# Starting the head mixing of an mLSTM layer at the first half of value chunk 0 instead of its second half

## The chip, the cores and the metric

The kernel runs on one core of one Trainium2 chip. The metric is the device time of one execution in microseconds. Engines are named as in the profile: PE (matrix products), PEld (its weight loads), DVE (elementwise work), ACT (activations and copies), POOL, and SP (which issues most transfers). Each engine works through its own instructions in the order in which the program lists them; semaphores hold an instruction back until what it needs is done.

## The reference

A trunk of two layers on 256 tokens of width 2048. The change lies in the second layer, an mLSTM with 8 heads (key width 128, value width 256):

```python
u = hn @ o_w_in[j]                      # q and k (2048), v (2048), og (2048), z (2048), gates (16)
qk = jax.nn.silu(causal_conv(qk, c_conv_w[j], c_conv_b[j]))
li = ig + c_b_i[j]
lf = jax.nn.log_sigmoid(fg + c_b_f[j])
yc = mlstm(q, k, v, li, lf)             # per head: exp-weighted causal q k^T, times v, with a normaliser
yc = head_rmsnorm(yc, c_norm[j]) * jax.nn.sigmoid(og) * jax.nn.silu(z)
h = h + yc @ o_w_out[j]
```

The kernel does the recurrence as one full causal product per head: scores q k^T, weighted by exponentials of gate sums, then times v. Products in 32-bit precision are made of three reduced-precision products of a high part ("hi") and a rest ("lo") of each operand.

## The kernel before

**Weight products.** Each projection is cut into chunks of 512 columns. `seven` (L288) makes two chunks at a time, with a Strassen-like scheme of seven products on the first quarter of the rows and plain products on the other three. It is a generator; it holds four PSUM banks A, F, B (pool `pm`, tile name `mm`, three banks) and E (pool `px`, name `mx`, three banks) and works through a string of operations, `a5a6.2aA7b.4F.bb`. `a` and `b` are plain products of 24 matmuls (`plain`), a digit is one Strassen product of 6, a dot is a call of `pump`, and `A` and `F` hand the first and the second half (128 tokens each) of the first chunk to the caller; E and B follow at the end as the halves of the second chunk. Ahead of the string stand two products of 6, into A and then into E. Three passes matter here: pass 1 is `seven(a["ov"], 0, ...)` for value chunks 0 and 1, pass 2 `seven(a["ov"], 2, ...)` for value chunks 2 and 3, pass 3 the first of the output gate, on `in_oog_dram`. All these matmuls are recorded at L235 (`product`). The first matmul of every product is tied by `tc.issue_after(last["pe"])` to stand behind the last matmul of the product before it, so the products never change places among themselves. Weights come through raw buffers; ACT makes the hi part (`whi`, L137 or L221), DVE the lo part (`wlo`, L138 or L222), in four buffers each.

**Lanes.** Other work hangs in named lanes, each a queue of generators. `pump` (L77) takes one step of each lane; it is called in the middle of each `plain` and at each dot. `drain` runs a lane to its end at once. The framework's scheduler then settles, when the program is built, in which order each engine's instructions stand: in general as they were written, earlier ones or those under `high_priority` first, and an instruction that needs a buffer stands behind those whose buffer it takes over.

**The lanes here.** `qk0` to `qk3` hold `features(t, j)` (L1196): convolution and SiLU of the q and k chunks, on DVE at L1218 (taps) and L1222, and on ACT at L1221 (`th`, the tanh). Lane `mix` holds `gate_stats` (L1256; it ends in eight small transposes `aT<-ae` at L1285), then `mix(0)` to `mix(3)` (two heads each) and `mix_norm`. One `mix(j)` consists of these steps, a step for each `pump`:

1. "spread": two PE matmuls (L431) broadcast a row of gate maxima over a bank `mx`; DVE subtracts it (`wt`, L1305 and L1306), ACT takes exponentials (L1310, L1311).
2. hi and lo parts of q and k (`qhl`, `khl`; ACT L1322, DVE L1323). `khl` lies in tag `th` of pool `tp`, two buffers that it shares with the `th` of `features`. For j = 0 there is one idle step ahead of this.
3. "scores": six matmuls L1329 and two L1330 into two banks `mx`; DVE multiplies them into `wt` (L1331); ACT makes `sh` (L1334), DVE `sl` (L1335).
4. "nu": 18 matmuls L1349 of `sh`/`sl` with the value tiles `vt`/`vl` of chunk j, into two banks `mx` and two `st`; then copies, row sums and squares (L1352, L1353, L1355). The next `mix` begins in the same step with its spread.

`px` has three banks. They go round in the order of the code: E of a pass, spreads, scores and two of the four nu banks all take their turn.

**Where the change acts.** `values` (L1386) takes the halves that passes 1 and 2 hand out, scales them into `vt` and `vl` (ACT L1394, DVE L1395), and at one of them puts `mix(0)` to `mix(3)` and `mix_norm` into their lane.

Of the kernel before, what the change touches and what calls it, by code (L numbers as in the profile page):

```python
# [45 lines left out]
def trunk(ctx: ExitStack, tc: tile.TileContext, a, out):  # L46
# [19 lines left out]
    def start(lane, gen):  # L66
        lanes.setdefault(lane, []).append(gen)
# [16 lines left out]
    def drain(*which):  # L84
        for lane in which:
            while step(lane):
                pass
# [687 lines left out]
    if True:  # L775
# [283 lines left out]
        vts = []  # L1059
# [133 lines left out]
    with tc.tile_pool(name="m1", bufs=2) as m1:  # L1193
# [50 lines left out]
        vts = []  # L1244
# [113 lines left out]
        def mix_norm():  # L1358


            t, r, yh = (m1.tile([P, 16], F32, name=n, bufs=1) for n in ("nwt", "nwr", "nwy"))
            s.activation(den, den, AF.Abs)
            v.tensor_tensor(out=den.rearrange("p (h n) -> p h n", h=2), in0=den.rearrange("p (h n) -> p h n", h=2),
                            in1=aT[:, 1, :, 0:8], op=ALU.max)
            v.tensor_scalar(den, den, 1e21, EPS ** 0.5, op0=ALU.min, op1=ALU.mult)
            v.tensor_tensor(out=den, in0=den, in1=den, op=ALU.mult)
            v.scalar_tensor_tensor(den, ss, 1.0 / 256, den, op0=ALU.mult, op1=ALU.add)
            newton(den, t, r, yh)
            for hf in range(2):
                c = slice(hf * 8, hf * 8 + 8)  # L1370
                v.tensor_scalar(fac[:, c], r[:, c], 0.5, None, op0=ALU.mult)
            yield
# [4 lines left out]
        def value_halves():  # L1377
            drain("combos")
            pr = pieces(m1.tile([P, 1024], F32, name="pr", tag="vt", bufs=6))
            yield from seven(a["ov"], 0, acth, qs, (0,), chain, pr, acc=True)  # L1380
            drain("spill")
            store_of.extend(hp.tile([P, 1024], F32, name="pr", tag="h") for _ in range(2))
            for b, hf, src in seven(a["ov"], 2, acth, qs, (0,), chain, part, acc=True):
                yield 2 + b, hf, src

        def values():  # L1386
            for j, hf, src in value_halves():
                if hf == 0:
                    vt = m1.tile([P, 2, 2, VW], F32R, name="vt", tag="vt", bufs=6)
                    gp.memset(vt.bitcast(F32)[:, :, :, 256:VW], 1.0)  # L1390
                    vl = ap.tile([P, 1024], F32R, name="vl", tag="ahl").rearrange("p (h i e) -> p h i e", h=2, i=2)
                with tc.high_priority(offset=450):
                    src = src.rearrange("p (i e) -> p i e", i=2)
                    s.activation(vt[:, hf, :, 0:256], src, AF.Copy, scale=norm["rt"][:, hf:hf + 1])  # L1394
                    v.scalar_tensor_tensor(vl[:, hf], src, norm["rt"][:, hf:hf + 1], vt[:, hf, :, 0:256].bitcast(F32),  # L1395
                                           op0=ALU.mult, op1=ALU.subtract)
                if hf == 0:
                    continue
                vts.append((vt, vl))
                if j == 0:  # L1400
                    drain("qk0", "qk2")
                    for c in range(4):
                        start("mix", mix(c))
                    start("mix", mix_norm())
# [18 lines left out]
        def mixed_gates():  # L1423
            for j, th in [x for x in held if x[0] in nums]:
                v.scalar_tensor_tensor(nums[j], th, 1.0, nums[j], op0=ALU.add, op1=ALU.mult)
            held[:] = [x for x in held if x[0] not in nums]

        values()
        for jj in (0, 2):
            ths = [m1.tile([P, 2, 512], F32, name="tho", tag="vt", bufs=6) for _ in range(2)]  # L1430
# [10 lines left out]
        for jj in (0, 2):  # L1441
            us = [m1.tile([P, 2, 512], F32, name="u", tag="vt", bufs=6) for _ in range(2)]
            for b, hf, src in pair(a["oz"], jj, True):
                j, u = jj + b, us[b]
# [292 lines left out]
```

## Time and profile before

| what | value |
|---|---|
| median of 3 runs | 1028.01 us (1027.76 to 1029.28) |
| the profiled execution | 1028.51 us |
| its span, first to last instruction | 1026.7 us |
| PE busy | 1011.9 us of the span |
| DVE, ACT, POOL busy | 850.5, 665.8, 103.5 us |
| HBM traffic | 236 GB/s over the span |

Start and launch around the span make up the 1.8 us between the first two profiled figures. The median of the runs lies 0.5 us under the profiled execution. In the timeline a row gives the start, the length, the engine, the line, the operation, and in brackets how long the engine had been idle and who released it. Instructions of one engine overlap by a little, so the distance between two starts is what one costs in a sequence.

### The profile page before, as it was taken

What the parts mean: (1) busy time and instruction counts of PE and PEld (TensorE: products, weight loads), DVE (VectorE), ACT (ScalarE), POOL (GpSimd) and SP (SyncE); (2) the same over time, 40 slices, a digit from 0 to 9 for tenths busy, and PEclk for the clock granted to TensorE, in tenths of its full rate; (3) what the DMA queues carried; (4) which work ended last, traced back from release to release, by engine and by line L of the source; (5) the groups of instructions that cost most, each with busy time, mean ns of one, the idle gap of its engine ahead of it and who ended that gap; (6) DMA issues with size and microseconds to landing.
All of it is one profiled execution on the core that took longest, in us unless ns stands there. A gap on an engine that the chain in (4) does not pass through costs nothing.

```text
span 1026.7 us, 14530 instructions
## 1 busy us (share of the span) xinstructions
PE 1011.9 (99%) x5152; PEld 838.6 (82%) x5152; DVE 850.5 (83%) x1242; ACT 665.8 (65%) x956; POOL 103.5 (10%) x184
## 2 busy tenths in 40 slices
PE   9999999999999999999999999899999999999996
PEld 8888888888888888878888877688888888888886
DVE  7858968969686888879579998778989997899794
ACT  7775554686974555567557877676666867465562
POOL 0111101011111111022021100000011110111000
PEclk9999999999999999999999999899999999999998
DMA  9987756567688799588897856447879889686852
GB/s 360 335 223 250 222 175 203 167 200 238 221 263 303 246 298 286 165 263 254 290 314 217 263 166 219 163 155 204 251 194 296 237 236 354 198 284 210 283 184 83
DMA packets 69960, 243.18 MB, mean 237 GB/s; under 512 B 9056, under 2 KB 10464, under 8 KB 69888
## 3 DMA queue, kind: packets, MB, share of 16 engines
q1 hardware_dynamic: 55872, 197.56, 57.5%
q0 software_dynamic: 13584, 44.18, 16.4%
q8 instruction: 40, 0.66, 0.3%
q10 hardware_dynamic: 432, 0.52, 0.1%
q14 instruction: 32, 0.26, 0.1%
HBM read 222.31 MB, written 19.92 MB: 236 GB/s over the span
## 4 chain that ended last, share of the span: by engine, by line
PE 89%; DVE 7%; issue 1%; ACT 1%; DMA 1%; ACTq 0%; DVEq 0%; POOLq 0%
PE mm L235 27%; PE mm L211 12%; PE mm L213 12%; PE mm L212 12%; PE mx L235 8%; PE mx L213 3%; PE mx L212 3%; PE mx L211 3%; DVE wlo L138 2%; DVE qk L1218 2%; DVE wlo L222 1%; PE mm L517 1%; PE nu L1349 1%; PE mx L517 1%; PE mm L1562 1%
## 5 line engine op out<-in xcount | busy, mean ns | idle before, releaser
L138 DVE TENSOR_TENSOR wlo<-raw,whi 128x1024 fp32r<-128x1024 f32 (+1 forms) x305 | 366.1, 1211 | 101.8 <-ACT whi L137 96.2
L137 ACT CAST whi<-raw 128x1024 fp32r<-128x1024 f32 (+1 forms) x305 | 318.0, 1046 | 202.5 <-PE mm L213 84.4
L235 PE MATMUL mm<-whi,ahl 128*128 128x512 f32 x804 | 258.4, 390 | 0.0
L211 PE MATMUL mm<-whi,ahl 128*128 128x512 f32 x576 | 225.3, 392 | 0.0
L212 PE MATMUL mm<-wlo,ahl 128*128 128x512 f32 x576 | 224.2, 389 | 0.0
L213 PE MATMUL mm<-whi,ahl 128*128 128x512 f32 x576 | 224.1, 389 | 0.0
L235 PEld LDWEIGHTS mm<-whi,ahl 128*128 128x128 f32 x804 | 150.7, 188 | 31.1
L235 PE MATMUL mm<-wlo,ahl 128*128 128x512 f32 x402 | 156.7, 390 | 0.0
L211 PEld LDWEIGHTS mm<-whi,ahl 128*128 128x128 f32 x576 | 108.1, 188 | 23.0 <-issue 0.4
L213 PEld LDWEIGHTS mm<-whi,ahl 128*128 128x128 f32 x576 | 108.1, 188 | 22.5
L212 PEld LDWEIGHTS mm<-wlo,ahl 128*128 128x128 f32 x576 | 108.2, 188 | 22.0
L222 DVE TENSOR_TENSOR wlo<-ch,whi 128x1024 fp32r<-128x1024 f32 x73 | 88.2, 1219 | 11.3 <-ACT whi L221 9.6
L221 ACT CAST whi<-ch 128x1024 fp32r<-128x1024 f32 x73 | 76.2, 1049 | 26.4 <-PE mm L235 13.9
L235 PEld LDWEIGHTS mm<-wlo,ahl 128*128 128x128 f32 x402 | 75.5, 188 | 15.5
L235 PE MATMUL mx<-whi,ahl 128*128 128x512 f32 x216 | 71.3, 390 | 0.0
L235 PE MATMUL mm<-whi,q 128*128 128x512 f32 x156 | 53.1, 390 | 0.0
L211 PE MATMUL mx<-whi,ahl 128*128 128x512 f32 x128 | 49.8, 389 | 0.0
L212 PE MATMUL mx<-wlo,ahl 128*128 128x512 f32 x128 | 49.8, 389 | 0.0
L213 PE MATMUL mx<-whi,ahl 128*128 128x512 f32 x128 | 49.8, 389 | 0.0
L235 PEld LDWEIGHTS mx<-whi,ahl 128*128 128x128 f32 x216 | 40.5, 188 | 8.7 <-issue 0.4
L235 PE MATMUL mx<-wlo,ahl 128*128 128x512 f32 x108 | 42.2, 391 | 0.0
L235 PEld LDWEIGHTS mm<-whi,q 128*128 128x128 f32 x156 | 29.3, 188 | 6.2
(389 smaller groups left out, 1344.7 us busy)
## 6 DMA issues: line engine op xcount, KB each, us to landing
raw<-in_ew_dram SPq DMA_DIRECT2D x64, 512.0 KB, 4.9
raw<-in_g_dram SPq DMA_DIRECT2D x60, 512.0 KB, 4.6
raw<-in_oqk_dram SPq DMA_DIRECT2D x32, 512.0 KB, 5.2
raw<-in_eo_dram SPq DMA_DIRECT2D x30, 512.0 KB, 4.9
raw<-in_oo_dram SPq DMA_DIRECT2D x30, 512.0 KB, 6.6
raw<-in_ov_dram SPq DMA_DIRECT2D x26, 512.0 KB, 4.6
raw<-in_oog_dram SPq DMA_DIRECT2D x24, 512.0 KB, 4.5
raw<-in_oz_dram SPq DMA_DIRECT2D x20, 512.0 KB, 4.5
```

Of the source, the lines that this page charges most:

```text
L137: last["act"] = s.copy(h, r).ins
L138: last["dve"] = v.tensor_tensor(out=l, in0=r, in1=h.bitcast(F32), op=ALU.subtract).ins
L211: te.matmul(ps[hf], xh, wh, start=(k == 0), stop=False, skip_group_check=True)
L212: te.matmul(ps[hf], xh, wl, start=False, stop=False, skip_group_check=True)
L213: last["pe"] = te.matmul(ps[hf], xl, wh, start=False, stop=(k == KT - 1), skip_group_check=True).ins
L221: last["act"] = s.copy(hi, r).ins
L222: last["dve"] = v.tensor_tensor(out=lo, in0=r, in1=hi.bitcast(F32), op=ALU.subtract).ins
L235: last["pe"] = te.matmul(o, x, y, start=(first and k + i == 0), stop=(end and k == n - 1 and i == 2), skip_group_check=True).ins
L517: last["pe"] = te.matmul(ps[hf][:, o:o + w_], tokens(pact[x], k, hf), (hi, lo)[y][:, k * 512 + o:k * 512 + o + w_], start=(n == mine[0]), ...
L1218: v.scalar_tensor_tensor(dst[:, sh:T], pi[:, 0:T - sh], pc("ccw", k * 16 + n), dst[:, sh:T], op0=ALU.mult, op1=ALU.add)
L1349: te.matmul(ps[:, 0:n], x[:, i, o:o + P], y[:, b, i], start=(b == 0 and x is sh and y is vh), stop=(b == hf and y is vl))
L1562: te.matmul(o, xh, wl, start=False, stop=False)
```

## The change

The condition in `values` is turned round. Before, the block that drains lanes `qk0` and `qk2` and starts the `mix` generators ran at the second half of value chunk 0 (operation `F` of pass 1); now it runs at its first half (operation `A`). The list `vts`, which `mix` waits for ahead of its nu step, still grows at second halves alone. No computation is added or left out.

```diff
@@ -1394,10 +1394,9 @@
                     s.activation(vt[:, hf, :, 0:256], src, AF.Copy, scale=norm["rt"][:, hf:hf + 1])
                     v.scalar_tensor_tensor(vl[:, hf], src, norm["rt"][:, hf:hf + 1], vt[:, hf, :, 0:256].bitcast(F32),
                                            op0=ALU.mult, op1=ALU.subtract)
-                if hf == 0:
-                    continue
-                vts.append((vt, vl))
-                if j == 0:
+                if hf:
+                    vts.append((vt, vl))
+                elif j == 0:
                     drain("qk0", "qk2")
                     for c in range(4):
                         start("mix", mix(c))
```

Between `A` and `F` lie two calls of `pump` (inside the first `b`, and at a dot). `gate_stats` ends at the first of them, so in that call `mix(0)` already takes its first step, and every later step of the lane comes two calls earlier than before, until `mix(2)` waits one call for its value chunk. The steps thus move against the passes: scores(0) goes from pass 2's first `a` to pass 1's next-to-last operation, nu(0) and spread(1) from pass 2's second `a` to pass 1's last `b`, that is, ahead of the code that takes bank E for pass 2. The three places that follow show the order that results.

PE at the border between pass 1 and pass 2. The first row is the end of pass 2's product into A, the rows `mx<-whi,q` are pass 2's product into E, and `mm<-whi,ahl` behind them is pass 2's first `a`. Before:

```order
L235 MATMUL mm<-wlo,ahl 128x512
L235 MATMUL mm<-whi,ahl 128x512
L235 MATMUL mx<-whi,q_5090 128x512
L235 MATMUL mx<-wlo,q_5090 128x512
L235 MATMUL mx<-whi,q_5090 128x512 x2
```

Now the same place (only the head of the 18 nu matmuls is shown; E's product, as in the rows above, stands behind the last of them):

```order
L235 MATMUL mm<-wlo,ahl 128x512
L235 MATMUL mm<-whi,ahl 128x512
L1329 MATMUL mx<-qhl,khl 128x256 x4
L1330 MATMUL mx<-qk 128x128
L1329 MATMUL mx<-qhl,khl 128x256 x2
L1330 MATMUL mx<-qk 128x128
L1349 MATMUL nu<-vt,sh 128x258 x4
L431 MATMUL mx<-s_5488,identr 128x256 x2
L1349 MATMUL nu<-vt,sl 128x258
L1349 MATMUL nu<-vl,sh 128x256
```

Scores(0), nu(0) and spread(1), which stood 80 and more weight matmuls further on, now all stand between pass 2's product into A and its product into E.

DVE at the same place, behind the transposes and L1305 of `mix(0)`. The tile `qk_5649` is the q and k chunk of `features` in lane `qk3`, `khl_5691` is the k operand of scores(0), `khl_5899` that of scores(1), and `wlo_5917` is a weight part for pass 2's operation `5`. Now:

```order
L1306 TENSOR_TENSOR wt_5629<-cst_85,mx_5626 128x2x128
L1218 SCALAR_TENSOR_TENSOR qk_5649<-xr_5648,prm_84,qk_5649 128x254
L222 TENSOR_TENSOR wlo_5917<-ch_5847,whi_5916 128x1024
L1218 SCALAR_TENSOR_TENSOR qk_5649<-xr_5648,prm_84,qk_5649 128x253
L310 TENSOR_TENSOR ch_5847<-ch_5847,ch_5862 128x1024
L1222 SCALAR_TENSOR_TENSOR qk_5649<-th_5660,qk_5649 128x512
L1218 SCALAR_TENSOR_TENSOR qk_5649<-xr_5676,prm_84,qk_5649 128x255 x2
L1218 SCALAR_TENSOR_TENSOR qk_5649<-xr_5676,prm_84,qk_5649 128x254 x2
L1218 SCALAR_TENSOR_TENSOR qk_5649<-xr_5676,prm_84,qk_5649 128x253 x2
L1222 SCALAR_TENSOR_TENSOR qk_5649<-th_5687,qk_5649 128x512
L1323 TENSOR_TENSOR khl_5691<-qk_5457,khl_5691 128x256
L1323 TENSOR_TENSOR khl_5899<-qk_5457,khl_5899 128x256
```

Before, the same feature work and the lo part of k (there `khl_5751`) were spread between weight parts:

```order
L1218 SCALAR_TENSOR_TENSOR qk_5639<-xr_5666,prm_84,qk_5639 128x253
L1218 SCALAR_TENSOR_TENSOR qk_5639<-xr_5666,prm_84,qk_5639 128x255
L1305 TENSOR_TENSOR wt_5683<-cst_85,mx_5680 128x2x256
L1218 SCALAR_TENSOR_TENSOR qk_5639<-xr_5666,prm_84,qk_5639 128x254
L138 TENSOR_TENSOR wlo_5991<-raw_5989,whi_5990 128x1024
L1323 TENSOR_TENSOR qhl_5750<-qk_5147,qhl_5750 128x512
L138 TENSOR_TENSOR wlo_5997<-raw_5995,whi_5996 128x1024
L1218 SCALAR_TENSOR_TENSOR qk_5639<-xr_5666,prm_84,qk_5639 128x253
L222 TENSOR_TENSOR wlo_6047<-ch_5797,whi_6046 128x1024
L138 TENSOR_TENSOR wlo_6059<-raw_6057,whi_6058 128x1024
L1323 TENSOR_TENSOR khl_5751<-qk_5457,khl_5751 128x256
```

The two `L1222` and the six taps in one run are now all ahead of the lo part of k, and no weight part for pass 2's second `a` is among them.

ACT at the same place, now; `th_5660` and `th_5687` are the two tanh tiles of lane `qk3`, whose buffers `khl_5691` and `khl_5899` take over:

```order
L1310 ACTIVATE wt_5629<-wt_5629,aT_5343 128x256 x2
L345 COPY mm_5845<-mm_5844 128x512
L221 CAST whi_5916<-ch_5847 128x1024
L1311 ACTIVATE wt_5629<-wt_5629,aT_5343 128x128 x2
L1221 ACTIVATE th_5660<-qk_5649 128x512
L1221 ACTIVATE th_5687<-qk_5649 128x512
L1322 CAST khl_5691<-qk_5457 128x256
L1322 CAST khl_5899<-qk_5457 128x256
L1334 CAST sh_5732<-wt_5629 128x768
```

The hi part of k stands directly behind both tanhs; before (`khl_5751`) it stood behind both too, but eleven instructions, seven of them weight casts, lay between the two tanhs. Passes 2 and 3 also meet in another way: before, nu(2) and spread(3) stood between pass 3's product into A and its product into E; now those two products follow each other, scores(3) stands in pass 2's last `b`, and nu(3) in pass 3's operation `5`. PE's order is the same again from about the middle of pass 3.

## The prediction

> **What bounds the kernel now.** I read the page's head first.
>
> ```profile
> span 1026.7 us, 14530 instructions
> PE 1011.9 (99%) x5152; PEld 838.6 (82%) x5152; DVE 850.5 (83%) x1242; ACT 665.8 (65%) x956; POOL 103.5 (10%) x184
> PE 89%; DVE 7%; issue 1%; ACT 1%; DMA 1%; ACTq 0%; DVEq 0%; POOLq 0%
> ```
>
> PE is busy 99% of the span and carries 89% of the chain that ended last. The change takes no matmul away, so it can act only through PE's idle time, 14.8 us in all, and through PE's clock. The view of waits lists what PE waited for; these four rows are those of the head mixing:
>
> ```profile
> PE nu L1349 <- ACT sh L1334: 4.4, 1, 4.4
> PE mx L431 <- DVE s L426: 0.8, 1, 0.8
> PE mx L1329 <- ACT khl L1322: 0.2, 1, 0.2
> PE mx L1329 <- DVE khl L1323: 0.2, 1, 0.2
> ```
>
> One wait is large. The busy time by windows (length, then PE, PEld, DVE, ACT, POOL, the granted clock, the DMA share) shows what stands around it:
>
> ```profile
> 625.00:659.00 34.00, 33.53 (x175) 27.18 (x174) 28.65 (x46) 24.74 (x56) 0.11 (x1) 1.00 0.52 171
> 659.00:664.00 5.00, 0.65 (x3) 0.25 (x3) 3.84 (x5) 2.54 (x4) 0.00 (x0) 0.81 0.60 192
> 664.00:668.50 4.50, 4.50 (x21) 4.50 (x22) 2.28 (x5) 2.86 (x9) 0.00 (x0) 0.50 0.37 140
> ```
>
> After the wait PE runs 4.5 us at half its clock. PE's timeline gives the marks that I count from:
>
> ```profile
> 606.36 0.39 PE L235 MATMUL mm<-whi,ahl 128*128 128x512 f32 x1
> 606.59 0.39 PE L235 MATMUL mx<-whi,q 128*128 128x512 f32 x1
> 624.72 0.61 PE L235 MATMUL mm<-whi,ahl 128*128 128x512 f32 x2
> 637.37 0.49 PE L431 MATMUL mx<-s,identr 128*128 128x256 f32 x2
> 637.70 0.40 PE L235 MATMUL mm<-wlo,ahl 128*128 128x512 f32 x1
> 659.06 0.39 PE L235 MATMUL mm<-whi,ahl 128*128 128x512 f32 x1
> 663.80 1.20 PE L1349 MATMUL nu<-vt,sh 128*128 128x258 f32 x4 [4.35 <-ACT sh L1334]
> 668.30 0.63 PE L235 MATMUL mx<-whi,q 128*128 128x512 f32 x1
> 669.98 0.39 PE L235 MATMUL mm<-whi,ahl 128*128 128x512 f32 x1
> 680.67 0.28 PE L1349 MATMUL nu<-vt,sh 128*128 128x258 f32 x1
> 682.82 0.39 PE L235 MATMUL mm<-whi,ahl 128*128 128x512 f32 x1
> ```
>
> 606.36 is the last matmul of pass 2's product into A, 606.59 the first of its product into E, and 668.30 the first of pass 3's product into E. From 606.59 to 624.72 PE does 80 weight matmuls (6 into E, 24 of `a`, 6 of `5`, 24 of `a`, 6 of `6`, 6 of `2`, 8 of `a`) without a gap: 0.227 us each. The 18 nu matmuls from 680.67 to 682.82 take 2.15 us at full clock.
>
> **The change, part by part.** *What now stands at 606.59.* The order puts scores(0), nu(0) and spread(1) between the product into A and the product into E. No other weight product can pass them: each is tied behind the one before, and E's bank is the one that spread(1) gives back. So from 606.75, where the last matmul of A ends, PE waits for all that scores(0) and nu(0) need. I follow that chain through DVE and ACT, with the distance between starts from these rows:
>
> ```profile
> 603.58 0.48 DVE L1285 STREAM_TRANSPOSE aT<-ae 32x64 f32<-32x64 f32 x2
> 609.30 0.48 DVE L1218 SCALAR_TENSOR_TENSOR qk<-xr,prm,qk 128x254 f32<-128x254 f32 x1
> 609.70 1.22 DVE L222 TENSOR_TENSOR wlo<-ch,whi 128x1024 fp32r<-128x1024 f32 x1
> 610.84 0.47 DVE L1218 SCALAR_TENSOR_TENSOR qk<-xr,prm,qk 128x253 f32<-128x253 f32 x1
> 611.23 1.22 DVE L310 TENSOR_TENSOR ch<-ch 128x1024 f32<-128x1024 f32 x1
> 612.36 1.22 DVE L138 TENSOR_TENSOR wlo<-raw,whi 128x1024 fp32r<-128x1024 f32 x1
> 613.50 0.68 DVE L1222 SCALAR_TENSOR_TENSOR qk<-th,qk 128x512 f32<-128x512 f32 x1
> 614.10 0.48 DVE L1218 SCALAR_TENSOR_TENSOR qk<-xr,prm,qk 128x255 f32<-128x255 f32 x1
> 620.22 0.68 DVE L1305 TENSOR_TENSOR wt<-cst,mx 128x512 f32<-128x512 f32 x1
> 622.35 0.69 DVE L1323 TENSOR_TENSOR qhl<-qk,qhl 128x512 fp32r<-128x512 f32 x1
> 627.68 0.42 DVE L1306 TENSOR_TENSOR wt<-cst,mx 128x256 f32<-128x256 f32 x1
> 628.30 0.42 DVE L1323 TENSOR_TENSOR khl<-qk,khl 128x256 fp32r<-128x256 f32 x1 [0.20 <-ACT khl L1322]
> 628.64 1.19 DVE L1331 SCALAR_TENSOR_TENSOR wt<-mx,wt 128x384 f32<-128x384 f32 x2
> ...
> 624.60 0.64 ACT L1221 ACTIVATE th<-qk 128x512 f32<-128x512 f32 x1 [0.27 <-DVE qk L1218]
> 625.14 0.39 ACT L1322 CAST khl<-qk 128x256 fp32r<-128x256 f32 x1
> 630.70 0.84 ACT L1334 CAST sh<-wt 128x768 fp32r<-128x768 f32 x1
> ```
>
> Consecutive rows give 0.40 for L1218, 1.14 for L138, L222 and L310, 0.60 for L1222; by the same overlap of 0.08, 0.60 for L1305 and qhl, 0.34 for L1306 and khl.
>
> - DVE does what it did up to 603.58, then seven transposes (0.24 each): 605.3.
> - L1305 0.60, L138 1.14, qhl 0.60, L138 1.14, L1306 0.34: 609.1. All they wait for (spread(0), the hi parts on ACT) is there earlier.
> - L1218, L222, L1218, L310, L1222: 0.40 + 1.14 + 0.40 + 1.14 + 0.60 = 3.7, so 612.8; then six taps, 2.4: 615.2, the last ending at 615.3.
> - ACT's second tanh waits for that tap: 0.64, to 615.95. The hi part of k follows, as its buffer is the tanhs' and ACT keeps its order: 0.39, to 616.3. The first two score matmuls can start there.
> - DVE: the second L1222 616.0 to 616.7, the lo part of k to 617.0. The other score matmuls, at half clock, end at about 618.2; L1331 follows each bank, the second ending at 618.8; sh takes 0.84: 619.7.
> - 18 nu and two spread matmuls at half clock, as from 663.80 to 668.30: 4.3 to 4.5 us. E's product starts at about **624.0** instead of 606.59: 17.4 later. I take 0.3 more for its six matmuls while the clock is still half (668.30 to 669.98 is 1.68, where six of 0.227 are 1.36).
>
> *What leaves its old place.* From 624.72 to 637.37 PE did 35 weight matmuls (16 rest of `a`, 6 of `7`, 13 of `b`), 7.93 us; the other 4.72 were scores(0), nu(0) and their seams and small waits. With spread(1), 637.37 to 637.70, 5.05 us go.
>
> *The later wait.* Before, nu(2) stood between the products into A and E of pass 3, behind this:
>
> ```profile
> 662.19 0.55 DVE L1331 SCALAR_TENSOR_TENSOR wt<-mx,wt 128x384 f32<-128x384 f32 x1
> 662.82 0.83 ACT L1334 CAST sh<-wt 128x768 fp32r<-128x768 f32 x1 [1.81 <-DVE wt L1331]
> ```
>
> Now these two products meet; scores(3) has 12 matmuls of B behind it, nu(3) 24 of `a` and half of `5`, and nu(2) has 18 between it and its scores. The wait goes: 659.06 + 0.23 to 663.80 is 4.5; the half clock, 4.50 against 2.15 + 0.33 = 2.0; E's six matmuls 0.3. Together 6.8 us. What is late next: DVE comes out of the first wait with pass 2's weight parts to do, but their four buffers come free only as PE moves on, so it can be kept waiting for PE there and catches up. Following the new order with the same durations I find nu(1) to nu(3) ready 1 to 2 us ahead of PE, nu(3) by the least. Bounds: none of the 6.8 comes back, or all.
>
> *Other queues.* POOL's fill of `vt` of chunk 1 moves behind two of its transfers, and SP issues two loads for pass 3 earlier; both are needed over 5 us later. Chunk 1's eviction (L1394, L1395) moves behind L1305 of `mix(1)`, to 622 to 624; only the copy into B waits for it, which PE needs in the second half of `a`, 2.7 us after E's product. That costs nothing while PE is itself late; without this cover it would be 1 to 2 us.
>
> Sum: 17.4 + 0.3 − 5.05 − 6.8 = **+5.9 us**. The profiled execution took 1028.51 us, 1.8 more than its span, so 1034.4; the median of the runs is 0.5 lower, and from it I come to 1033.9, say **1034**.
>
> The half clock rests on the rows 659 to 668.5 (0.50 after an idle 4.35 us). The Trainium skill, "TensorE: Matmul & The Clock Gate", Part 1, says that about 3.4 us of idle time halve the clock and about 3.4 us of sustained work restore it. By that page, as an estimate, if the short burst of scores counted towards the 3.4 us, part of nu(0) would run at full clock and the sum would be about 1.5 us lower; the trace's own stretch was 4.5 us or more.
>
> **The rivals.**
>
> *Faster: the first wait stays short.* The mixing's inputs are early, PE stops little at 606.75, and the later wait goes. For it: the large wait and its half clock are real and are taken away. Against it: the order of ACT and DVE, in which k's parts stand behind both tanhs. Price: if k came right behind L1306, sh would be done near 612.7 and E would start near 615.2 at full clock: 8.6 − 5.05 − 6.8 = −3.3, so 1024.7; with no wait at all −6.8, 1021. It decides in favour of faster if E's product starts before 606.59 + 11.9 = 618.5.
>
> *No difference.* The same point, hit within 2 us: the first wait about two thirds of what I reckon. DVE would have to do its twenty-three instructions from 603.58 to the last tap in under 8 us, where the rows give 11.7.
>
> *Slower still: both waits.* The first as reckoned, and one of 4 us plus half clock near nu(2), nu(3) or pass 3's E, since DVE carries over its arrears: 17.7 − 5.05 = +12.7, so 1041.
>
> *The change does nothing.* The order shows it moving the matmuls, so I give that no chance of its own.
>
> **How the numbers follow.** A measurement of this kernel can tell about 0.2%, 2 us, from no change. My forecast, 1034 with a range of its own of 1031.5 to 1037, has 0.73; both waits 0.10; no difference 0.08; faster 0.09. The range that should hold 8 times in 10 runs from 1031 to 1041: the forecast, and the slower rival at its top. Slower by over 0.2%: 0.83; within: 0.08; faster: 0.09.
>
> **What would show it.** In the changed profile: PE idle for 9 to 10 us from 606.75 with khl (L1322) as releaser, again 1 to 2 us ahead of nu with sh (L1334); the granted clock near 0.5 from there to about 624; no wait over 1 us at pass 3's first products, where the clock stays at 1.0; DVE running the six L1218 in one piece ahead of khl. I am wrong if E's product of pass 2 starts before 618, if a wait of 4 us is left near pass 3, or if weight casts (L137, L221) hold PE up after the first wait.

## The result, and the profile after

| what | before | after |
|---|---|---|
| median of 4 runs each, on one chip | 1028.30 us (1027.76 to 1029.28) | 1035.07 us (1034.12 to 1035.85) |
| ratio, 95% interval | 1 | 1.0064 (1.0047 to 1.0082) |
| the profiled execution | 1028.51 us | 1035.12 us |
| its span | 1026.7 us | 1033.3 us |

The changed kernel is 0.64% slower. By the medians that is 6.8 us, between the two profiled executions 6.6 us; the prediction had 5.9 against the profiled execution, and 1034 us. The head of the changed kernel's page:

```profile
span 1033.3 us, 14519 instructions
...
PE 1012.0 (98%) x5152; PEld 839.0 (81%) x5152; DVE 850.6 (82%) x1242; ACT 665.9 (64%) x956; POOL 103.2 (10%) x184
...
PE 94%; DVE 4%; issue 1%; ACT 1%; DMA 0%; ACTq 0%; POOLq 0%
```

PE's busy time is the same to 0.1 us and so is its count of instructions. The span grew by 6.6 us of idle time. That PE's share of the chain rises from 89% to 94% is no sign of a better kernel: the chain only leaves PE where PE waits, and it now does so at another place. What PE waits for in the changed kernel (total, times, longest):

```profile
PE mx L1329 <- ACT khl L1322: 9.5, 1, 9.5
PE nu L1349 <- issue: 1.6, 1, 1.6
PE mx L431 <- DVE s L426: 0.8, 1, 0.8
```

The 4.4 us of nu for sh are gone, and in their place stand 9.5 us of scores(0) for khl and 1.6 us ahead of nu(0). The profile puts the second one down to "issue", but ACT's sh ends only 0.1 us before PE goes on, as the rows further down show. Busy time by windows of the changed kernel (length, PE, PEld, DVE, ACT, POOL, granted clock, DMA share, GB/s):

```profile
606.50:625.00 18.50, 7.42 (x32) 7.00 (x32) 15.16 (x29) 8.35 (x18) 1.12 (x4) 0.65 0.36 86
625.00:659.00 34.00, 34.00 (x168) 28.53 (x168) 22.70 (x32) 24.55 (x51) 0.00 (x0) 0.99 0.56 186
659.00:664.00 5.00, 5.00 (x30) 4.21 (x29) 4.88 (x8) 3.50 (x6) 0.00 (x0) 1.00 0.52 165
664.00:668.50 4.50, 4.50 (x23) 3.76 (x23) 2.24 (x6) 4.46 (x15) 0.00 (x0) 1.00 0.52 168
668.50:690.00 21.50, 21.50 (x109) 18.10 (x108) 19.34 (x26) 14.52 (x27) 0.00 (x0) 1.00 0.53 175
```

From 625 to 690 PE is now busy throughout, at a clock of 0.99 to 1.00. That stretch holds the meeting of passes 2 and 3, which cost the kernel before its wait and its half clock (659 to 668.5) and which now comes later, near 676. All the loss lies between 606.5 and 625, where PE works 7.42 us of 18.5. The clock of 0.65 is the mean of that whole stretch, the idle time included; while nu(0) runs it is 0.50:

```profile
621.00:624.50 3.50, 3.50 (x18) 3.50 (x17) 2.72 (x6) 2.72 (x6) 0.10 (x1) 0.50 0.02 5
```

PE's timeline at this place, and at pass 3:

```profile
606.21 0.39 PE L235 MATMUL mm<-whi,ahl 128*128 128x512 f32 x1
616.12 1.35 PE L1329 MATMUL mx<-qhl,khl 128*128 128x256 f32 x4 [9.52 <-ACT khl L1322]
...
618.12 0.63 PE L1330 MATMUL mx<-qk 128*128 128x128 f32 x2
620.30 1.20 PE L1349 MATMUL nu<-vt,sh 128*128 128x258 f32 x4 [1.56 <-issue]
...
624.52 0.42 PE L1349 MATMUL nu<-vl,sh 128*128 128x256 f32 x1
624.73 0.63 PE L235 MATMUL mx<-whi,q 128*128 128x512 f32 x1
...
626.51 0.39 PE L235 MATMUL mm<-whi,ahl 128*128 128x512 f32 x1
...
676.17 0.39 PE L235 MATMUL mx<-whi,q 128*128 128x512 f32 x1
```

The last matmul of pass 2's product into A starts at 606.21, and the product into E at 624.73; before, these two stood 0.23 us apart. In pass 3 E's product, at 676.17, follows without a gap. DVE in the changed kernel, between the two:

```profile
603.43 1.73 DVE L1285 STREAM_TRANSPOSE aT<-ae 32x64 f32<-32x64 f32 x7
...
608.67 0.41 DVE L1306 TENSOR_TENSOR wt<-cst,mx 128x256 f32<-128x256 f32 x1
...
612.66 2.44 DVE L1218 SCALAR_TENSOR_TENSOR qk<-xr,prm,qk 128x255 f32<-128x255 f32 x6
615.80 0.69 DVE L1222 SCALAR_TENSOR_TENSOR qk<-th,qk 128x512 f32<-128x512 f32 x1 [0.70 <-ACT th L1221]
616.41 0.98 DVE L1323 TENSOR_TENSOR khl<-qk,khl 128x256 fp32r<-128x256 f32 x2
...
618.78 0.56 DVE L1331 SCALAR_TENSOR_TENSOR wt<-mx,wt 128x384 f32<-128x384 f32 x1 [0.30 <-PE mx L1330]
```

And ACT in the changed kernel:

```profile
615.14 0.63 ACT L1221 ACTIVATE th<-qk 128x512 f32<-128x512 f32 x1 [3.47 <-DVE qk L1218]
615.68 0.39 ACT L1322 CAST khl<-qk 128x256 fp32r<-128x256 f32 x1
...
619.37 0.83 ACT L1334 CAST sh<-wt 128x768 fp32r<-128x768 f32 x1 [2.44 <-DVE wt L1331]
```

Read the two together from the bottom: PE's scores start at 616.12 because the hi part of k ends at 616.07; that cast stands behind the second tanh; the tanh stands behind the six taps, which run in one piece on DVE until 615.10 and for which ACT had been idle 3.47 us. DVE itself had no pause from the transposes to there. The work was not slow, it was asked for too early.

### The profile page after: what moved, and what is told of

Read it like the earlier page. It is cut to its first block, busy times and chain, and to the rows that moved or that the text cites. A ratio compares the mean times of both kernels' runs of the same rounds, so it can differ in the third digit from the quotient of the medians.

```text
span 1033.3 us, 14519 instructions
## 1 busy us (share of the span) xinstructions
PE 1012.0 (98%) x5152; PEld 839.0 (81%) x5152; DVE 850.6 (82%) x1242; ACT 665.9 (64%) x956; POOL 103.2 (10%) x184
## 4 chain that ended last, share of the span: by engine, by line
PE 94%; DVE 4%; issue 1%; ACT 1%; DMA 0%; ACTq 0%; POOLq 0%
PE mm L235 29%; PE mm L211 13%; PE mm L212 13%; PE mm L213 13%; PE mx L235 8%; PE mx L211 3%; PE mx L213 3%; PE mx L212 3%; PE mm L517 1%; PE nu L1349 1%; DVE wlo L138 1%; DVE qk L1218 1%; PE mx L517 1%; PE mm L1562 1%; PE mm L1561 1%
```

## The experiments

The theory: PE's order is fixed, so what stands ahead of E's product holds up every weight product behind it. The first wait is the time DVE and ACT need for scores(0) and nu(0); the later wait of the kernel before had the same cause with nu(2). Each profiled execution reaches the spread of mix(0) at a time of its own (603.71 before, 603.56 after, up to 605.62 in others), from differences in the first microseconds. So between kernels I compare distances from that mark: from there to pass 2's E it is 606.59 − 603.71 = 2.9 us before and 624.73 − 603.56 = 21.2 after. From the same mark to the end of the span it is 1026.7 − 603.71 = 423.0 us before and 1033.3 − 603.56 = 429.7 after, so 6.7 us of the change's loss do not hang on the start.

### The later wait alone

Kernel before, with nu(2) two calls of `pump` later, which puts it and spread(3) behind E's product:

```diff
             while len(vts) <= j:
                 yield
+            if j == 2:
+                yield
+                yield
             vh, vl = vts[j]
```

> The kernel before, with two idle steps ahead of nu(2): passes 2 and 3 meet without it, pass 3's product into A is followed by its product into E, and everything ahead of nu(2) is as before. Theory (the later wait and its half clock cost 6.8 us, and nothing else gains in the change): no wait over 1 us near pass 3's first products, granted clock 1.0 there, 6 to 7 us faster than before: about 1021.5, ratio 0.9935. Rival (DVE's arrears near 660 only move the wait to the next mixing step): a wait of 3 us or more ahead of nu(2) or nu(3) in pass 3, time within 2 us of before.

Measured: 1021.81 us (1021.51 to 1022.68), ratio to before 0.9941 (0.9928 to 0.9953). The windows around the old wait, in this kernel:

```profile
659.00:664.00 5.00, 5.00 (x24) 4.14 (x23) 4.95 (x6) 4.28 (x6) 0.00 (x0) 1.00 0.57 189
664.00:668.50 4.50, 4.49 (x22) 3.55 (x21) 3.84 (x6) 2.96 (x4) 0.00 (x0) 1.00 0.71 238
```

No wait, full clock, and 6.0 us less than before in those runs (1027.85). From the spread to the end of the span it is 1020.9 − 604.33 = 416.6 us, 6.4 less than before. That is the prediction's term for the later wait, 6.8, paid out nearly whole, without the change. This kernel is faster than both. The edit moves more than nu(2) and spread(3), though: scores(3) and nu(3) come later too, and on DVE the eviction of value chunk 3 goes ahead of L1331 of `mix(2)`, so that sh is ready at 667.6 instead of 663.7. nu(2) starts at 667.77, as soon as that, but E's product no longer stands behind it.

Was it the place, or just the delay? The same edit with one `yield` instead of two asks for nu(2) a call later, but leaves it between the two products:

```diff
             while len(vts) <= j:
                 yield
+            if j == 2:
+                yield
             vh, vl = vts[j]
```

> The kernel before with one added call of waiting ahead of nu(2) instead of the two of e4_nu2_later. In the order PE's nu(2) then still stands between pass 3's products into A and E. Theory (the 4.4 us wait near pass 3 comes from that place alone, through bank E): the wait of nu for sh of about 4 us and the clock of about 0.5 behind it stay, and the time is that of before, 1028 within 1 us. Rival (any delay of nu(2) helps, since it gives DVE and ACT time): the time falls to 1022 to 1025.

Measured: 1028.32 us (1027.72 to 1029.96), ratio 1.0004 (0.9995 to 1.0014). Its wait, and the two windows:

```profile
PE nu L1351 <- ACT sh L1334: 4.4, 1, 4.4
```

```profile
659.00:664.00 5.00, 0.60 (x4) 0.21 (x3) 4.05 (x6) 2.91 (x5) 0.00 (x0) 1.00 0.59 207
664.00:668.50 4.50, 4.49 (x22) 4.14 (x23) 2.60 (x6) 2.86 (x9) 0.00 (x0) 0.62 0.32 123
```

The wait stays to a tenth (L1351 is nu there). In PE's order the added call moves scores(3) and nu(3), which stand behind nu(2); nu(2) itself keeps its place and starts at 663.91, where it started at 663.80 before. So a call of delay that does not change nu(2)'s place gains nothing, and the rival in that form falls. A nu(2) that starts later and still stands ahead of E's product was not tried. With e4_nu2_later, in which sh comes 4 us later and PE still does not wait, the runs show that it is the place ahead of E's product that costs.

### nu(0) behind E's product

Changed kernel; scores(0) stays ahead of E's product, nu(0) and spread(1) go behind it:

```diff
             while len(vts) <= j:
                 yield
+            if j == 0:
+                yield
             vh, vl = vts[j]
```

> The change with one more idle step ahead of nu(0), so that nu(0) and spread(1) stand behind pass 2's product into E and E's bank no longer hangs on them; scores(0) alone still stand ahead of that product. Theory (the wait is that of scores(0) for k's parts, behind both tanhs; the nu step only lengthens it): PE still stands idle for about 10 us or more behind pass 2's product into A, khl as releaser; the product into E starts near 620 instead of 624.7, but nu(0) and spread(1), 2.6 us, come later and the half clock falls on full weight products; the time stays within 1.5 us of the change's 1035, near 1034.5. Rival (what holds PE up is nu(0) and the bank that E takes over from spread(1)): the wait at that place falls below 3 us and the time to about 1024.

Measured: 1034.17 us (1033.35 to 1034.47), ratio 1.0057 (1.0041 to 1.0072) in runs with 1027.85 before: 6.3 us over before, where the changed kernel was 6.8 over. So taking nu(0) out of the way hardly helps. Its wait, and the start of E's product:

```profile
PE mx L1329 <- ACT khl L1322: 11.3, 1, 11.3
```

```profile
620.31 0.77 PE L235 MATMUL mx<-whi,q 128*128 128x512 f32 x1
```

The second wait is gone, and E's product starts 16.7 us behind the spread instead of 21.2. But its six matmuls now take 2.7 us, to 623.02, instead of 1.8, nu(0) and spread(1) still have to be done behind it, and the first wait is 1.8 us longer. DVE in this kernel shows why:

```profile
604.01 0.75 DVE L1397 SCALAR_TENSOR_TENSOR vl<-pr,rcr,vt 128x512 fp32r<-128x512 f32 x1
...
606.44 0.74 DVE L1397 SCALAR_TENSOR_TENSOR vl<-mm,rcr,vt 128x512 fp32r<-128x512 f32 x1
...
615.64 1.38 DVE L1218 SCALAR_TENSOR_TENSOR qk<-xr,prm,qk 128x253 f32<-128x253 f32 x3
```

With nu(0) later, the eviction of value chunk 1 (L1397 here) stands among the transposes again, ahead of scores(0), as in the kernel before; the last tap ends at 617.0 instead of 615.1. The edit moved more than its one step. The expected time came out, in part for another reason than I had in mind.

### The hi and lo parts of k one step earlier

Changed kernel, with the idle step of mix(0) behind the making of `qhl` and `khl` instead of ahead of it, so that k's parts stand behind the first tanh and not behind both:

```diff
             while 4 + j not in qk:
                 yield
-            if j == 0:
-                yield
             qhl = room2("qhl").rearrange("p (s i t) -> p s i t", s=2, i=2)
...
                     v.tensor_tensor(out=hl[:, 1], in0=src, in1=hl[:, 0].bitcast(F32), op=ALU.subtract)
+            if j == 0:
+                yield
             yield
```

> The change with the idle step of mix(0) moved from ahead of qhl/khl to behind it, so that khl stands behind the first tanh only, ahead of the six taps and the second tanh; PE's order is the same. Scores(0) can start near 612 instead of 616.1. Theory (the chain runs through DVE's queue: the six taps still stand ahead of the two L1331 that follow the scores): L1331 ends near 616.4 instead of 619.3, so nu(0) starts near 617.4 instead of 620.3 and the time falls by 2.9 us against the change, to about 1032. Rival (k's buffer behind the second tanh is the whole cost of the first wait): nu(0) near 614.5, 6 us or more against the change, 1029 or less.

Measured: 1032.20 us (1032.09 to 1032.31), ratio 1.0040 (1.0026 to 1.0054): 2.9 us under the changed kernel's 1035.07. PE's timeline in this kernel:

```profile
612.37 1.10 PE L1329 MATMUL mx<-qhl,khl 128*128 128x256 f32 x3 [5.44 <-ACT khl L1320]
...
617.69 1.20 PE L1349 MATMUL nu<-vt,sh 128*128 128x258 f32 x4 [2.73 <-issue]
...
622.12 0.63 PE L235 MATMUL mx<-whi,q 128*128 128x512 f32 x1
```

The wait for khl falls from 9.5 to 5.4 us, and 1.2 of those 4.1 us come back ahead of nu(0): DVE does L1331 from 615.71 on, behind the six taps, where the scores end at 614.96. From the spread to E it is 18.2 us, 3.0 less than in the changed kernel. The theory's numbers came out (2.9 us less, L1331 as the brake), and the rival falls. Of the first wait some 4 us thus come from the second tanh, behind which `khl` stands in the changed kernel. The other 5.4 us end with the first tanh, at 611.39, which waits for a tap on DVE until 611.36. The run moves the code and not the buffer: that `khl` stands behind the tanhs because it takes over their buffers is read from the order and not shown by itself, and a buffer of its own for `khl` was not tried.

### Both edits at once

The edits of the last two experiments together, on the changed kernel:

```diff
-            if j == 0:
-                yield
             qhl = room2("qhl").rearrange("p (s i t) -> p s i t", s=2, i=2)
...
+            if j == 0:
+                yield
             yield
...
             while len(vts) <= j:
                 yield
+            if j == 0:
+                yield
```

> The changed kernel with both edits of e6_khl_early (k's hi and lo parts a call earlier) and e3_nu0_later (nu(0) and spread(1) a call later, behind E's product). Theory (the first wait has two parts in a row, khl for the scores and sh for nu(0), both only because the work stands ahead of E's product): PE waits about 5.4 us for khl, starts scores(0) at 612.4 and E's product at 614.9, 7.2 earlier than in e6_khl_early, and does nu(0) and spread(1) later at full clock for 2.5 us: 1032.2 - 7.2 + 2.5 = 1027.5. Rival (DVE's arrears set the time behind the wait, so an earlier E only moves the waiting to weight parts): new waits for wlo or whi of 3 us or more and a time above 1030.

Measured: 1031.10 us (1030.49 to 1034.51), ratio 1.0030 (1.0020 to 1.0040). Neither was right. The time is above 1030, as the rival had it, but its waits for weight parts did not come, so its reason falls. And the first wait was not the 5.4 us on which the theory counted:

```profile
PE mx L1329 <- ACT khl L1320: 8.7, 1, 8.7
```

DVE in this kernel, and the first tanh on ACT:

```profile
603.68 0.76 DVE L1397 SCALAR_TENSOR_TENSOR vl<-pr,rcr,vt 128x512 fp32r<-128x512 f32 x1
...
606.11 0.75 DVE L1397 SCALAR_TENSOR_TENSOR vl<-mm,rcr,vt 128x512 fp32r<-128x512 f32 x1
...
612.74 2.05 DVE L1218 SCALAR_TENSOR_TENSOR qk<-xr,prm,qk 128x254 f32<-128x254 f32 x5
```

```profile
614.03 0.63 ACT L1221 ACTIVATE th<-qk 128x512 f32<-128x512 f32 x1 [1.62 <-DVE qk L1218]
```

The eviction of chunk 1 is ahead of scores(0) again. The hi part of k, for which PE waits, stands behind the first tanh, and this one starts 10.7 us behind the spread where it was 7.5 in e6_khl_early: besides the eviction (1.5 us), L310 (1.1 us) and a third tap (0.4 us) now stand ahead of it on DVE, where e6_khl_early had two taps. The wait is 3.3 us longer than assumed and the time 3.6 us over the expected 1027.5. What follows the wait agrees with the theory: against e6_khl_early E's product starts 4.2 us sooner behind the spread (14.0 instead of 18.2), its six matmuls take 0.9 us more at half clock, and nu(0) and spread(1) cost 2.4 us behind it; that leaves 0.9 us less, and the measured time is 1.1 less. The mechanism held, the order that I took for granted did not. I had added up two edits without reading the order of their sum.

### The half clock behind the first wait

Changed kernel, with 36 matmuls that nobody uses, on `qhl` into a bank of tag `st`, written ahead of scores(0), so that PE does not rest while it waits:

```diff
             yield
+            if j == 0:
+                fl = pst.tile([P, 512], F32, name="fl", tag="st")
+                for n in range(36):
+                    te.matmul(fl, qhl[:, 1, 0, 0:P], qhl[:, 1], start=(n == 0), stop=(n == 35))
             for i in range(2):
```

> The change with 36 added matmuls of the q operand's rest with itself into an unused PSUM bank, ahead of scores(0); nothing reads them, and no engine's order changes else. They take 36 x 0.227 = 8.2 us, from 607.7 (their operand) to 615.9, inside PE's first wait. Theory (half clock on top of the wait): the wait's end stays at khl, 616.1; scores(0), nu(0), spread(1) and the product into E run at full clock; pass 2's product into E starts near 621.9 instead of 624.7 and the time falls by 3.3 us against the change, to 1031.5 to 1032. Rival (all that follows is set by ACT and DVE, the clock costs little): less than 1 us against the change, 1034 or more.

Measured: 1033.80 us (1032.93 to 1034.72), ratio 1.0056 (1.0042 to 1.0069): 1.3 us under the changed kernel by the medians of four runs each, whose ranges overlap, and between the two expectations. PE's timeline, ACT's hi part of k, and a window, in this kernel (L1333 is the scores, L1353 is nu):

```profile
608.34 8.47 PE L1328 MATMUL fl<-qhl 128*128 128x512 f32 x36 [1.10 <-DVE qhl L1323]
616.79 1.16 PE L1333 MATMUL mx<-qhl,khl 128*128 128x256 f32 x5
...
620.26 0.71 PE L1353 MATMUL nu<-vt,sh 128*128 128x258 f32 x4 [1.68 <-issue]
...
622.99 0.39 PE L235 MATMUL mx<-whi,q 128*128 128x512 f32 x1
```

```profile
616.35 0.39 ACT L1322 CAST khl<-qk 128x256 fp32r<-128x256 f32 x1
```

```profile
606.50:625.00 18.50, 15.69 (x79) 12.55 (x78) 15.93 (x31) 10.09 (x22) 1.13 (x4) 1.00 0.34 87
```

The clock stayed at 1.00, and nu(0) with spread(1) took 622.99 − 620.26 = 2.73 us, against 624.73 − 620.30 = 4.43 in the changed kernel. From the spread (604.23 here) to E's product it is 18.8 us, 2.4 less than in the changed kernel, and from the spread to the end of the span 1031.1 − 604.23 = 426.9, 2.9 less: in this execution the half clock was worth about what the theory had. I compared the end of the filling, 616.8, with the 616.1 at which khl was ready in the changed kernel, took it to be 0.7 us late, and tried 30 matmuls:

```diff
-                for n in range(36):
-                    te.matmul(fl, qhl[:, 1, 0, 0:P], qhl[:, 1], start=(n == 0), stop=(n == 35))
+                for n in range(30):
+                    te.matmul(fl, qhl[:, 1, 0, 0:P], qhl[:, 1], start=(n == 0), stop=(n == 29))
```

> The run e5_fill with 30 unused matmuls instead of 36, since with 36 the filling ended about 0.7 us after khl was ready and held the scores back. Begun at 608.3 and 0.227 us each it ends at 615.2, ahead of khl. Theory (the half clock behind the first wait costs about 3 us: scores(0), nu(0) and spread(1) at full clock): scores start at 616.1 as in the changed kernel, nu(0) near 619.7, E's product near 622.1 instead of 624.7, and the time near 1032, 3 us under the changed kernel. Rival (the clock is worth no more than the 1.2 us that e5_fill gained, since PE has slack behind E that takes up an earlier E): E comes earlier, yet the time is at 1033.5 or above.

Measured: 1035.47 us (1034.05 to 1037.43), ratio 1.0068 (1.0047 to 1.0089). The changed kernel itself, run again beside it:

> The changed kernel itself, unaltered, for a comparison with the three that follow: 1035 us by every theory, with E's product of pass 2 near 624.7 in its profile.

Measured: 1035.08 us (1034.02 to 1035.80), ratio 1.0062 (1.0047 to 1.0078). So 30 matmuls gained nothing, and the reason for trying them was wrong: e5_fill reached its spread 0.67 us later than the changed kernel did, and in its own rows the hi part of k ends at 616.35 + 0.39 = 616.74 and the scores start at 616.79, so the 36 matmuls held nothing back. With 30, PE rests again ahead of the scores. PE's timeline in the kernel with 30 (its spread stands at 605.62, 2.06 us later than in the changed kernel):

```profile
609.73 7.09 PE L1328 MATMUL fl<-qhl 128*128 128x512 f32 x30 [1.10 <-DVE qhl L1323]
618.17 1.15 PE L1333 MATMUL mx<-qhl,khl 128*128 128x256 f32 x5 [1.35 <-ACT khl L1322]
...
621.63 1.20 PE L1353 MATMUL nu<-vt,sh 128*128 128x258 f32 x4 [1.68 <-issue]
...
626.06 0.63 PE L235 MATMUL mx<-whi,q 128*128 128x512 f32 x1
```

Here the clock did not hold. Scores(0) ran at full clock (its first five matmuls in 1.15 us, where four took 1.35 in the changed kernel), but nu(0) ran at half: 4.43 us again. From the spread to E it is 20.4 us, 0.7 less than in the changed kernel, all of it from the scores. The rival's number came out (1033.5 or above with an earlier E), but this run cannot bear out its reason, since the clock it was to keep was lost ahead of nu(0). What the half clock costs the changed kernel is thus seen in one execution, the profiled one of e5_fill: 1.7 us on nu(0) and spread(1), 0.9 on the scores, 0.4 on E's product, 2.9 in all from the spread to the end. The medians show 1.3 us of it, and the other executions were not profiled, so whether the full 3 us can be had every time stays open.

## Why the prediction was right

**PE bounds, and only its idle time and clock can act.** Right: 1012.0 us busy against 1011.9.

**Term 1, the chain ahead of E's product (+17.4, +0.3).** Right in its links up to khl, 0.9 us too short at its end. The changed trace runs 0.15 us earlier than the one of before at the spread, so 0.15 is to be added to its times here. The last tap was reckoned to end at 615.3 (measured 615.1 + 0.15), the hi part of k at 616.3 (616.07 + 0.15), the second L1331 at 618.8 (619.34 + 0.15), sh at 619.7 (620.20 + 0.15), E at 624.0 (624.73 + 0.15). Up to khl the sum is right to 0.1. The miss of 0.7 arises in the scores: I let them take 1.9 us, from 616.3 to 618.2, but at half clock they take 2.63, from 616.12 to the end of the last matmul at 618.12 + 0.63 = 618.75. E's six matmuls took 626.51 − 624.73 = 1.78 us, 0.42 over the 1.36 of full clock, where I had 0.3.

**Term 2, what leaves its old place (−5.05)**, is not seen by itself in the changed trace, and no run moved it alone. It holds only as far as the sum below closes.

**Term 3, the later wait goes (−6.8).** Right: no wait and a clock of 0.99 to 1.00 from 625 to 690. e4_nu2_later, which takes this wait away without the change, gained 6.0 us by the medians and 6.4 from the spread to the end, a little less than 6.8; e4b_nu2_later keeps nu(2) in its place, and keeps the wait.

**The sum.** With the measured first term, 624.73 − 606.21 − 0.23 = 18.3, it is 18.3 + 0.4 − 5.05 − 6.8 = +6.9 us, against 6.6 between the profiled executions, 6.7 between them from the spread on, and 6.8 between the medians. The prediction's +5.9 was short by the end of term 1. The two halves of the change can now be told apart: taking the later wait away alone gains 6.0 us, the whole change loses 6.8, so what it puts at the first place costs 12.8 us, where 17.4 + 0.3 − 5.05 = 12.65 was reckoned. That this fits so well is partly luck: with the measured first term it would be 13.65, and the 1.0 us by which that term was too short nearly cancels the 0.8 by which e4_nu2_later stays below 6.8. From the spread on, the two halves are 6.4 and 13.1 us; the rest of about 0.5 us against 13.65 is open.

**The other queues.** The move of chunk 1's eviction (on DVE now from 623.5 to 624.9) cost PE no wait, and it is even what keeps the first wait at 9.5 us: with the eviction in its old place e3_nu0_later waits 11.3. I had counted that move only as harmless in the prediction, and missed it when I added the edits of e7_both.

**The half clock.** The scores filled 2.63 us, and nu(0) ran at half clock all the same, so the estimate of 1.5 us less, for the case that this burst counted as sustained work, did not come. The Trainium skill, "TensorE: Matmul & The Clock Gate", Part 1, asks for about 3.4 us of sustained work to restore the clock; with a burst of 2.63 us between two idle stretches the trace agrees.

**The rivals.** "Faster" turned on E starting before 618.5; it started at 624.73. The price worked out for k's parts standing right behind L1306, 1024.7 us, was put to no run; e6_khl_early moves them only part of the way. "No difference" asked DVE to do its twenty-three instructions up to the last tap in under 8 us; it took 615.10 − 603.43 = 11.7, as reckoned. "Both waits" fell: no wait came near pass 3, and no weight part held PE up after the first wait.

## What to carry to other kernels

Where one engine's order is fixed, ask of every piece that is moved which products come to stand behind it, and whether its inputs are then ready; how early it starts does not matter by itself. A wait of 4.4 us was worth removing, but by moving the one step that stood in the way (three added lines, 6 us gained), not by pulling its whole lane forward, which removed it and put 11 us of waiting at another place. And read the order of each combination of edits anew: the same step of delay moved an eviction on another engine too.

## What the runs showed of the hardware

The clock fell to half without any long rest. In e5b_fill30 PE rested 1.35 us, worked 1.8 us on the scores and rested 1.68 us; then nu(0) ran at half clock. In e5_fill the same 1.68 us, with some 10 us of work without a pause ahead of it (608.34 to 618.57), left the clock at 1.00. The Trainium skill, "TensorE: Matmul & The Clock Gate", Part 1, puts the fall down to an idle window of about 3.4 us that runs freely; no single rest here was half as long, so the measurement differs from that rule unless a window counts as idle that is partly busy, which no run here shows. The recovery varies too: after the same wait of 4.4 us, nu(2), spread(3) and E's start took 668.30 − 663.80 = 4.50 us in the kernel before, and in e4b_nu2_later it was 4.18 us (to E at 668.09), as the first four nu matmuls still ran partly at full clock and the last one did again:

```profile
663.91 0.89 PE L1351 MATMUL nu<-vt,sh 128*128 128x258 f32 x4 [4.39 <-ACT sh L1334]
...
667.74 0.28 PE L1351 MATMUL nu<-vl,sh 128*128 128x256 f32 x1
```

At half clock throughout the four take 1.20 us and a single one 0.42, as in the changed kernel's rows at 620.30 and 624.52.
